# Moving the log1p series of a hybrid decoder kernel from GpSimd to VectorE

## The chip, the cores and the metric

The kernel runs on one NeuronCore of a Trainium2 chip. The metric is the device time of one launch in microseconds (us). A core has five engines with a queue each, and each works through its queue in order: TensorE (PE, matmuls), VectorE (DVE), ScalarE (ACT), GpSimd (POOL) and SyncE (SP, here only a queue that issues DMAs). They wait for one another by semaphores.

## The reference

One inference step of a two-layer recurrent decoder, for a prompt of 512 tokens and 8 sample tokens with shared weights. Layer 0 has an RG-LRU branch and a Mamba-2 branch behind one input projection; layer 1 is HGRN2. The parts that matter here are two softplus expressions of layer 0:

```python
log_a = -LRU_C * r * jax.nn.softplus(-lam.astype(F32))
dt = jax.nn.softplus(b_dt.astype(F32) + b_dt_bias.astype(F32))
a_neg = -jnp.exp(b_a_log.astype(F32))
acs = jnp.cumsum(dtc * a_neg.reshape(G_B, hg), axis=2)
```

lam has 1024 entries (128 partitions x 8), dt has 16 heads for each token (128 x 80: five blocks of tokens by 16 heads). softplus(x) is max(x, 0) + log1p(exp(-|x|)), and log1p(z) is worked out as twice a series in s = z / (z + 2): s (1 + s²/3 + s⁴/5 + ... + s¹⁶/17).

## The kernel before

All 520 tokens stand along the free dimension and features along the partitions. Each projection takes a 128-column tile of weights, loads it as float32, and splits it into a high part (fp32r, `whi`, a cast on ACT or DVE) and a residual (`wlo`, a subtraction on DVE); three products (`xnh` by `whi`, `xnl` by `whi`, `xnh` by `wlo`) of eight 128-blocks each make one tile, in two halves of 260 tokens. The order of layer 0's projections is: `ax` (8 tiles, the LRU's x), `xbc` (12 tiles, the Mamba x, B and C), `z`, `ag`, `z1`, then the output projections `oa` and `ob` and the gate `pg`. Layer 1 follows from about 450 us on.

Around these the small work is woven in. `evac_ax` (line 1116) copies an `ax` tile from PSUM into `bcs`, does the four-tap convolution into `xa` (prompt tokens on DVE; the sample tokens start with a scaling on POOL, line 1121, and go on with three fused steps on DVE), and calls `gates` (line 1092). `gates` splits `xa` into `xg`, multiplies it with the block-diagonal gate weights (the matmuls named `g`), and makes `lr`, `lg` and `lt` with ACT functions whose scale and bias are the LRU constants `c4` and `nc4` (in the tile `lamt`). `lru` (line 1131) takes the square roots and runs the recurrence as a scan on DVE.

`tables` (line 991) prepares the LRU constants: |lam|, a negation, an exp made exact by five squarings (`accurate_exp`, line 972), the series (`log1p_of`, line 956), the maximum, the sum and two scalings. `ssd_start` (line 1225) projects dt, takes |dt| and exp on ACT, runs the series, the maximum, the add and the product with `aneg` into `dA`, and sums `dA` along the tokens with a triangular matmul into `acs`; the whole chunked Mamba scan and the sample states (`ssd_chunk`, `ssd_sample`) hang on `acs`. In both places every step but the reciprocal stands on POOL.

The order in which instructions stand on each engine is not that of the code. Every call is recorded with a priority (the position of the projection at which it stands, shifted by `side(...)`), and the class `Plan` then works through all of them with a list of charges: it moves a clock of its own for each engine, gives each engine the ready instruction of the lowest priority number, and charges it. Lines 90 to 95 hold the charges that matter: DVE's fused step and tensor_tensor 0.067 + n/960 us, POOL's tensor_tensor 0.21 + n/480 and tensor_scalar 0.22 + n/1200, and `SYNC` (0.12 us, line 40) between a step and one that needs it. `later(4.0)` on line 1265 adds 4 us for TensorE work of `ssd_start` that waits for another engine. The chip then runs each queue in the order so found, whatever the true durations are. All of the instructions carry line 520 in the profile, since they are issued from there; they are told apart by their tiles. `dtt` holds dt's tiles, `htmp` the series' temporaries, `hb` holds `aneg`, `csm` is the sample part of the Mamba convolution, `smp` the sample states.

Of the kernel before, what the change touches and what calls it, by code (L numbers as in the profile page):

```python
# [21 lines left out]
MUL, ADD, SUB, MAX, MIN = ALU.mult, ALU.add, ALU.subtract, ALU.max, ALU.min  # L22
# [7 lines left out]
NH = 16  # L30
# [179 lines left out]
class Plan:  # L210
# [53 lines left out]
    @contextmanager  # L264
    def block(self, main=False):

        self.open = Op(self, self.pos + self.shift, 0)
        self.open.forms["pe"] = [[], 0.0, None]
        self.open.main = main
        self.open.ins, self.open.outs = [], []  # L270
        yield
        op, self.open = self.open, None
        op.forms["pe"][1] /= 2400.0
        self.add(op, op.ins, op.outs)
# [266 lines left out]
def hybrid_decode_step_kernel(ctx: ExitStack, tc: tile.TileContext, I, O, mode="both"):  # L541
# [19 lines left out]
    act, dve, pool, pe, sp = (Engine(plans, k) for k in ("act", "dve", "pool", "pe", "sp"))  # L561
    side, block = (lambda *a, **k: plans[-1].side(*a, **k)), (lambda *a: plans[-1].block(*a))

    def new(pool_, shape, tag, name, bufs=1, dt=F32):
        return plans[-1].tile(pool_, shape, dt, tag, name, bufs, {"psm": PSUM, "psa": PSUM, "drp": DRAM}.get(pool_, SBUF))
# [7 lines left out]
    def grab(name):  # L573

        return new("psa", [128, 512], "ax", name)
# [7 lines left out]
    def bc(ap, shape):  # L583
        return ap.to_broadcast(shape)

    def tt(out, a, b, op, eng=dve):
        eng.tensor_tensor(out=out, in0=a, in1=b, op=op)

    def stt(out, a, s, b, op0, op1):
        dve.scalar_tensor_tensor(out=out, in0=a, scalar=s, in1=b, op0=op0, op1=op1)  # L590

    def ts(out, a, s1, op0, s2=None, op1=None, eng=dve):
        if op1 is None:
            eng.tensor_scalar(out=out, in0=a, scalar1=s1, scalar2=None, op0=op0)
        else:
            eng.tensor_scalar(out=out, in0=a, scalar1=s1, scalar2=s2, op0=op0, op1=op1)

    def fn(out, in_, func, **kw):
        act.activation(out, in_, func, **kw)

    def copy(out, in_):

        plans[-1].record(("act", "copy", (out, in_), {}), ("dve", "tensor_copy", (out, in_), {}))
# [9 lines left out]
    def ltile(shape, name, dt=F32):  # L613
        return new("lay", shape, name, name, dt=dt)
# [147 lines left out]
    htmp = new("big", [128, 4160], "h", "htmp")  # L762
# [38 lines left out]
    def select(t, pattern, base, cm, fill):  # L801
        pool.affine_select(out=t, in_=t, pattern=pattern, compare_op=ALU.is_ge, fill=fill, base=base,
                           channel_multiplier=cm)
# [29 lines left out]
    def P1(r, n=1):  # L833
        return pt[:, 0, r:r + n]

    def P2(r, n=1):
        return pt[:, 1, r:r + n]
# [108 lines left out]
    lamt = ltile([128, 4, 8], "lamt")  # L946
    c4, nc4 = lamt[:, 2], lamt[:, 3]
    hbias = ltile([128, 16], "hbias")
    hcn = ctile([128, NH], "hcn")
    aneg = hb[:, 2, :]  # L950
# [2 lines left out]
    flag = ctile([1, 1], "flag", I32)  # L953
    fl = ctile([128, 4], "fl")

    def log1p_of(z, n, lo):

        t = htmp[:, lo:lo + 4 * n].rearrange("p (a b) -> p a b", a=4)
        s, s2, q, r = t[:, 0], t[:, 1], t[:, 2], t[:, 3]
        ts(s, z, 2.0, ADD, eng=pool)  # L960
        dve.reciprocal(q, s)
        tt(s, z, q, MUL, pool)
        tt(s2, s, s, MUL, pool)
        ts(q, s2, 1.0 / 17.0, MUL, 1.0 / 15.0, ADD, pool)
        for c in (13, 11, 9, 7, 5, 3, 1):
            tt(q, q, s2, MUL, pool)
            ts(q, q, 1.0 / c, ADD, eng=pool)
        tt(r, q, s, MUL, pool)
        ts(r, r, 2.0, MUL, eng=pool)
        return r  # L970

    def accurate_exp(t, k):

        fn(t, t, AF.Exp, scale=1.0 / (1 << k))
        for _ in range(k):
            tt(t, t, t, MUL, pool)

    def buffers():

# [11 lines left out]
    def tables():  # L991
        pool.memset(triu, 1.0)
        select(triu, [[1, 128]], 0, -1, 0.0)

        act.activation(lamt[:, 0], P1(56, 8), AF.Abs)
        ts(lamt[:, 0], lamt[:, 0], -1.0, MUL, eng=pool)
        accurate_exp(lamt[:, 0], 5)
        l1p_ = log1p_of(lamt[:, 0], 8, 320)
        ts(lamt[:, 1], P1(56, 8), -1.0, MUL, 0.0, MAX, pool)
        tt(lamt[:, 1], lamt[:, 1], l1p_, ADD, pool)  # L1000
        ts(c4, lamt[:, 1], -4.0, MUL, eng=pool)
        ts(nc4, lamt[:, 1], 4.0, MUL, eng=pool)
        ts(hbias, P1(40, 16), 0.5, MUL, eng=pool)
        ts(hcn, P2(64, 16), 0.5, MUL, eng=pool)

        ts(P1(64, 60), P1(64, 60), 0.5, MUL, eng=pool)

    def dt_tables():
        pool.tensor_copy(aneg, hb[:, 1, :])
        accurate_exp(aneg, 5)  # L1010
        ts(aneg, aneg, -1.0, MUL, eng=pool)
        copy(dtws[:, :, :NH], dtw)
        tt(dtws[:, :, NH:], dtw, dtws[:, :, :NH].bitcast(F32), SUB)
# [46 lines left out]
    with plans[-1].together(xnl[:, 3]):  # L1060
        with side(12.0):
            buffers()
            tables()
        with side(25.0):
            dt_tables()
        with side(40.0):
            lower_bounds()
# [122 lines left out]
    dt_raw, dt_z, dt, dA, nacs = (dtt[:, i] for i in range(5))  # L1190
# [12 lines left out]
    def dt_project():  # L1203


        ps = [grab(f"dt{h_}") for h_ in range(2)]
        with block():
            for k in range(KT):
                for x in (xnh, xnl):
                    for h_ in range(2):  # L1210
                        pe.matmul(ps[h_][:2 * NH, :HN], lhsT=dtws[:, k, :], rhs=x[:, k, h_ * HN:(h_ + 1) * HN],
                                  start=(k == 0 and x is xnh), stop=(k == KT - 1 and x is xnl))
        dth = htmp[:2 * NH, 1888:1888 + N]
        for h_ in range(2):
            copy(dth[:, h_ * HN:(h_ + 1) * HN], ps[h_][:2 * NH, :HN])
        psd = grab("dtT")
        with block():
            for i in range(5):
                t0 = i * 128 if i < 4 else N - 128
                pe.transpose(psd[:, i * 2 * NH:(i + 1) * 2 * NH], dth[:, t0:t0 + 128], ident[:2 * NH, :2 * NH])  # L1220
        d3, p3 = dt_raw.rearrange("p (i h) -> p i h", i=5), psd[:, :160].rearrange("p (i a h) -> p i a h", i=5, a=2)
        tt(d3, p3[:, :, 1], bc(hb[:, 0, :].unsqueeze(1), [128, 5, NH]), ADD)
        tt(d3, p3[:, :, 0], d3, ADD)

    def ssd_start():
        dt_project()
        act.activation(dt_z, dt_raw, AF.Abs)
        fn(dt_z, dt_z, AF.Exp, scale=-1.0)
        lg_ = log1p_of(dt_z, 80, 0)
        ts(dt, dt_raw, 0.0, MAX, eng=pool)  # L1230
        tt(dt, dt, lg_, ADD, pool)
        tt(dA.rearrange("p (i h) -> p i h", i=5), dt.rearrange("p (i h) -> p i h", i=5),
           bc(aneg.unsqueeze(1), [128, 5, NH]), MUL, pool)
        ps = grab("acs")
        with block():
            pe.matmul(ps[:, 0:64], lhsT=triu, rhs=dA[:, :64], start=True, stop=True)
            pe.matmul(ps[:, 64:128], lhsT=ones, rhs=dA[:, :64], start=True, stop=True)
        copy(at_[:, 0:2, :], ps[:, :128].rearrange("p (a b) -> p a b", a=2))
        ts(nacs[:, :64], acs, -1.0, MUL)
        tt(edt, alast, acs, SUB)  # L1240
        ps = grab("acsT")
        with block():
            pe.transpose(ps[:64, :128], acs, ident)
            pe.transpose(ps[:16, 128:256], dt[:, 64:80], ident)
            pe.transpose(ps[:16, 256:384], dA[:, 64:80], ident)
        copy(acsT, ps[:64, :128])
        copy(sdt[:, 0, :], ps[:16, 248:256])
        fn(sdt[:, 1, :], ps[:16, 376:384], AF.Exp)
        fn(edt, edt, AF.Exp)
        fn(eal, alast, AF.Exp)  # L1250
        sp.dma_start(out=acsT_d, in_=acsT)
        sp.dma_start(out=sdt_d, in_=sdt.rearrange("h a b -> h (a b)"))
        for e in range(2):
            sp.dma_start(out=sfm[e * 64:(e + 1) * 64].rearrange("p j a b -> p j (a b)"),
                         in_=sdt_d.rearrange("(j e) c -> e j c", e=2)[e].partition_broadcast(64))
# [9 lines left out]
    with side(DT_LATE), plans[-1].later(4.0):  # L1265
        ssd_start()
        lru_out()
# [997 lines left out]
```

## Time and profile before

| what | value |
|---|---|
| median of 3 runs | 1056.26 us (1055.57 to 1057.36) |
| the profiled execution | 1052.58 us, span 1050.9 us, mean granted clock 0.994 |
| PE | 1023.1 us, 97% of the span |
| DVE | 832.6 us, 79%, 1705 instructions |
| ACT | 630.8 us, 60%, 1482 instructions |
| POOL | 139.4 us, 13%, 241 instructions |

A row in order of time reads: start, duration, engine, line, operation, tile written <- tiles read, shapes (partitions x elements), count, and in brackets how long the engine had been idle and what ended that. A row of a group reads: busy time in all, mean ns of one, idle time ahead of it. Starts of DVE and ACT instructions overlap the ends of those before, so a duration is longer than the distance between two starts. A row of a stretch has the engines' busy times, and behind them the share of full speed that TensorE's clock was granted.

### The profile page before, as it was taken

Reading aid. Unit: us, or ns where it says so; the run is one execution under the profiler, and the core shown is the slowest. Engines: PE = TensorE matmul, PEld = TensorE weight load, DVE = VectorE, ACT = ScalarE, POOL = GpSimd, SP = SyncE. Lnnn points to the kernel's source line nnn. Section 1 sums busy time; section 2 is a strip of 40 time slices with the busy share of each in tenths; the row PEclk is TensorE's granted clock in tenths of the full one; section 3 lists DMA queues with packets and bytes.
Section 4 is the critical chain, followed back from the end, with each engine's and each line's share of the span. In section 5 each row is a group of like instructions: output and inputs, shape, how many; then the busy total and the mean of one; then the engine's idle time right before and its main releaser. Section 6 shows DMA issues by size and latency. Waiting matters only on the chain.

```text
span 1050.9 us, 21517 instructions
## 1 busy us (share of the span) xinstructions
PE 1023.1 (97%) x8427; PEld 1000.0 (95%) x8427; DVE 832.6 (79%) x1705; ACT 630.8 (60%) x1482; POOL 139.4 (13%) x241
## 2 busy tenths in 40 slices
PE   9989899999999999999999999999999999999995
PEld 8989899899999999999999999999999999999995
DVE  6789788998996656697989759698598979868853
ACT  6588876654673222365676726678268685764553
POOL 4635854100000000001000000001000000100000
PEclk9999999999999999999999999999999999999998
DMA  9712254336586223553353433433434443553311
GB/s 285 246 30 92 81 166 141 122 110 191 188 257 213 89 98 117 153 203 90 98 149 109 142 91 108 139 100 113 122 90 139 124 116 111 137 180 121 121 41 45
DMA packets 129957, 138.45 MB, mean 132 GB/s; under 512 B 13704, under 2 KB 111128, under 8 KB 129832
## 3 DMA queue, kind: packets, MB, share of 16 engines
q1 hardware_dynamic: 129464, 136.64, 42.6%
q8 instruction: 68, 1.11, 0.4%
q10 hardware_dynamic: 160, 0.30, 0.1%
q14 instruction: 41, 0.34, 0.1%
q0 software_dynamic: 224, 0.06, 0.0%
HBM read 111.71 MB, written 25.44 MB: 131 GB/s over the span
## 4 chain that ended last, share of the span: by engine, by line
PE 73%; DVE 10%; DMA 6%; ACT 4%; POOL 3%; issue 2%; SPq 0%; POOLq 0%; ACTq 0%; DVEq 0%
PE o L520 10%; PE sm L520 9%; PE q L520 9%; PE pg L520 9%; PE g L520 8%; PE ob L520 4%; PE sg L520 4%; PE xbc L520 2%; PE ax L520 2%; DVE wlo L520 2%; PE oa L520 2%; PE pl L520 2%; PE z L520 1%; DMA smp<-in_state_b_ssm_dram 1%; POOL csm L520 1%
## 5 line engine op out<-in xcount | busy, mean ns | idle before, releaser
L520 ACT CAST whir<-wraw 128x512 fp32r<-128x512 f32 (+1 forms) x121 | 96.3, 798 | 83.9 <-PE o L520 40.6
L520 DVE TENSOR_TENSOR wlor<-wraw,whir 128x512 fp32r<-128x512 f32 (+1 forms) x121 | 109.6, 910 | 12.5 <-ACT whir L520 12.1
L520 ACT CAST whi<-wraw 128x1024 fp32r<-128x1024 f32 (+1 forms) x56 | 57.8, 1032 | 48.6 <-PE ob L520 34.5
L520 POOL TENSOR_TENSOR at__1738<-at__1738,nhalf 128x4 f32<-128x4 f32 (+1 forms) x24 | 22.6, 942 | 461.5 <-DVE at__1738 L520 455.5
L520 DVE TENSOR_TENSOR wlo<-wraw,whi 128x1024 fp32r<-128x1024 f32 (+1 forms) x64 | 77.3, 1208 | 8.0 <-ACT whi L520 7.4
L520 PE MATMUL o<-ohl,whir 128*128 128x260 f32 x512 | 83.0, 284 | 0.0
L520 PEld LDWEIGHTS o<-ohl,whir 128*128 128x128 f32 x512 | 70.0, 188 | 0.9 <-issue 0.6
L520 PE MATMUL g<-xh,whir 128*128 128x260 f32 x256 | 54.6, 294 | 1.1 <-DVE l1a L520 1.1
L520 PE MATMUL q<-xh,whir 128*128 128x260 f32 x256 | 53.2, 289 | 0.0
L520 PE MATMUL q<-xh,wlor 128*128 128x260 f32 x256 | 51.5, 283 | 0.0
L520 PE MATMUL q<-xl,whir 128*128 128x260 f32 x256 | 51.4, 282 | 0.0
L520 PE MATMUL g<-xl,whir 128*128 128x260 f32 x256 | 51.4, 282 | 0.0
L520 PE MATMUL g<-xh,wlor 128*128 128x260 f32 x256 | 51.4, 282 | 0.0
L520 PE MATMUL o<-ohl,wlor 128*128 128x260 f32 x256 | 51.4, 282 | 0.0
L520 DVE TENSOR_TENSOR h<-h,o 128x520 f32<-128x520 f32 x40 | 27.8, 694 | 26.2 <-PE o L520 25.9
L515 ACT ACT_TABLE_LOAD x36 | 46.2, 1283 | 0.6
L520 PE MATMUL sm<-uh,whir 128*128 128x260 f32 x140 | 40.4, 289 | 1.8 <-DVE l1a L520 1.6
L520 PE MATMUL sm<-xh,whir 128*128 128x260 f32 x140 | 41.4, 296 | 0.0
L520 PEld LDWEIGHTS g<-xh,whir 128*128 128x128 f32 x256 | 39.2, 189 | 2.2 <-DVE l1a L520 1.3
L520 PE MATMUL sm<-xh,wlor 128*128 128x260 f32 x140 | 39.6, 283 | 0.3 <-DVE wlor L520 0.3
L520 PE MATMUL xbc<-xnh,whi 128*128 128x260 f32 x192 | 39.7, 289 | 0.0
L520 PE MATMUL sm<-xl,whir 128*128 128x260 f32 x140 | 39.6, 283 | 0.0
(609 smaller groups left out, 3594.2 us busy)
## 6 DMA issues: line engine op xcount, KB each, us to landing
wraw<-in_c_w_in_dram SPq DMA_DIRECT2D x32, 1024.0 KB
wraw<-in_ab_w_in_dram SPq DMA_DIRECT2D x15, 1024.0 KB
wraw<-in_ab_w_out_dram SPq DMA_DIRECT2D x8, 1024.0 KB
wraw<-in_ple_gate_dram SPq DMA_DIRECT2D x8, 1024.0 KB
wraw<-in_c_w_out_dram SPq DMA_DIRECT2D x8, 1024.0 KB
pl<-pl_d SPq DMA_DIRECT2D x2, 2080.0 KB
smp<-in_state_b_ssm_dram SPq DMA_DIRECT2D x8, 512.0 KB
acy<-acsT_d SPq DMA_DIRECT2D x8, 512.0 KB
```

The lines of the kernel that those rows point to most:

```text
L515: self.engines["act"].preload_act_table_set(SETS[table])
L520: getattr(f, name)(*a, **k)
```

## The change

`log1p_of`, which returned the logarithm, becomes `softplus_tail`, which adds it to a tile that already holds the maximum. Its Horner steps are fused: the product and the sum of one coefficient, two POOL instructions before, are one scalar_tensor_tensor on DVE, and the last doubling and the add are one as well. With the reciprocal it has 14 instructions. The maximum, dt's product with `aneg`, and in `tables` the negation, the squarings and the two scalings move to DVE too. `accurate_exp` takes the engine as an argument; its other two uses stay on POOL. Priorities, charges and the planner are as they were.

```diff
-    def log1p_of(z, n, lo):
-
-        t = htmp[:, lo:lo + 4 * n].rearrange("p (a b) -> p a b", a=4)
-        s, s2, q, r = t[:, 0], t[:, 1], t[:, 2], t[:, 3]
-        ts(s, z, 2.0, ADD, eng=pool)
-        dve.reciprocal(q, s)
-        tt(s, z, q, MUL, pool)
-        tt(s2, s, s, MUL, pool)
-        ts(q, s2, 1.0 / 17.0, MUL, 1.0 / 15.0, ADD, pool)
-        for c in (13, 11, 9, 7, 5, 3, 1):
-            tt(q, q, s2, MUL, pool)
-            ts(q, q, 1.0 / c, ADD, eng=pool)
-        tt(r, q, s, MUL, pool)
-        ts(r, r, 2.0, MUL, eng=pool)
-        return r
-
-    def accurate_exp(t, k):
+    def softplus_tail(dst, z, n, lo):
+
+        t = htmp[:, lo:lo + 3 * n].rearrange("p (a b) -> p a b", a=3)
+        s, s2, r = t[:, 0], t[:, 1], t[:, 2]
+        ts(s2, z, 2.0, ADD)
+        dve.reciprocal(r, s2)
+        tt(s, z, r, MUL)
+        tt(s2, s, s, MUL)
+        ts(r, s2, 1.0 / 17.0, MUL)
+        for c in (15, 13, 11, 9, 7, 5, 3):
+            stt(r, r, 1.0 / c, s2, ADD, MUL)
+        stt(r, r, 1.0, s, ADD, MUL)
+        stt(dst, r, 2.0, dst, MUL, ADD)
+
+    def accurate_exp(t, k, eng=pool):
 
         fn(t, t, AF.Exp, scale=1.0 / (1 << k))
         for _ in range(k):
-            tt(t, t, t, MUL, pool)
+            tt(t, t, t, MUL, eng)
...
         act.activation(lamt[:, 0], P1(56, 8), AF.Abs)
-        ts(lamt[:, 0], lamt[:, 0], -1.0, MUL, eng=pool)
-        accurate_exp(lamt[:, 0], 5)
-        l1p_ = log1p_of(lamt[:, 0], 8, 320)
-        ts(lamt[:, 1], P1(56, 8), -1.0, MUL, 0.0, MAX, pool)
-        tt(lamt[:, 1], lamt[:, 1], l1p_, ADD, pool)
-        ts(c4, lamt[:, 1], -4.0, MUL, eng=pool)
-        ts(nc4, lamt[:, 1], 4.0, MUL, eng=pool)
+        ts(lamt[:, 0], lamt[:, 0], -1.0, MUL)
+        accurate_exp(lamt[:, 0], 5, dve)
+        ts(lamt[:, 1], P1(56, 8), -1.0, MUL, 0.0, MAX)
+        softplus_tail(lamt[:, 1], lamt[:, 0], 8, 320)
+        ts(c4, lamt[:, 1], -4.0, MUL)
+        ts(nc4, lamt[:, 1], 4.0, MUL)
...
         dt_project()
         act.activation(dt_z, dt_raw, AF.Abs)
         fn(dt_z, dt_z, AF.Exp, scale=-1.0)
-        lg_ = log1p_of(dt_z, 80, 0)
-        ts(dt, dt_raw, 0.0, MAX, eng=pool)
-        tt(dt, dt, lg_, ADD, pool)
+        ts(dt, dt_raw, 0.0, MAX)
+        softplus_tail(dt, dt_z, 80, 0)
         tt(dA.rearrange("p (i h) -> p i h", i=5), dt.rearrange("p (i h) -> p i h", i=5),
-           bc(aneg.unsqueeze(1), [128, 5, NH]), MUL, pool)
+           bc(aneg.unsqueeze(1), [128, 5, NH]), MUL)
```

## The prediction

> **What bounds the kernel now.** The table of engines comes first, then the stretches: start and end, length, busy time of each engine, and behind these the clock granted to TensorE.
>
> ```profile
> PE 1023.1 (97%) x8427; PEld 1000.0 (95%) x8427; DVE 832.6 (79%) x1705; ACT 630.8 (60%) x1482; POOL 139.4 (13%) x241
> ```
>
> ```profile
> core 0: us, PE busy (x) PEld busy (x) DVE busy (x) ACT busy (x) POOL busy (x), PEclk, DMA share, GB/s
> 42.00:61.00 19.00, 15.93 (x124) 14.94 (x124) 13.30 (x33) 9.90 (x20) 14.10 (x38) 1.00 0.53 185
> 61.00:100.00 39.00, 39.00 (x325) 38.48 (x325) 35.91 (x76) 34.34 (x57) 16.26 (x23) 1.00 0.27 82
> 100.00:128.00 28.00, 24.73 (x206) 24.35 (x205) 20.79 (x28) 25.18 (x38) 22.09 (x45) 1.00 0.24 76
> 128.00:130.00 2.00, 2.00 (x16) 2.00 (x17) 1.43 (x5) 0.21 (x2) 0.31 (x2) 0.90 0.00 0
> 130.00:132.00 2.00, 2.00 (x11) 2.00 (x10) 2.00 (x4) 1.11 (x4) 0.89 (x1) 0.50 0.00 0
> 132.00:134.00 2.00, 2.00 (x14) 2.00 (x14) 2.00 (x3) 1.22 (x4) 2.00 (x1) 0.74 0.03 8
> 128.00:175.00 47.00, 47.00 (x384) 46.39 (x385) 40.63 (x62) 32.46 (x70) 22.41 (x34) 0.96 0.44 138
> 175.00:300.00 125.00, 122.93 (x1023) 115.48 (x1022) 116.49 (x234) 73.74 (x229) 11.09 (x17) 1.00 0.52 160
> 300.00:1050.00 750.00, 734.26 (x6091) 723.36 (x6089) 575.67 (x1223) 427.23 (x1018) 34.06 (x41) 0.99 0.41 124
> ```
>
> PE is the bound: all but 27.8 us of the span (1050.9 - 1023.1) are matmuls. A change can gain where PE stands still, and POOL's average of 13% hides that it is busy 14.10 of 19 us and 22.09 of 28 us in exactly the two stretches around the change, where PE loses 3.07 and 3.27 us. So I asked each engine's instructions, in order of time, what it waited for there. First the LRU constants (42 to 61):
>
> ```profile
> 41.12 0.24 POOL L520 TENSOR_SCALAR htmp<-lamt 128x8 f32<-128x8 f32 x1
> 54.75 1.22 POOL L520 TENSOR_SCALAR lamt<-lamt 128x8 f32<-128x8 f32 x2
> ```
>
> ```profile
> 51.75 0.25 DVE L520 SCALAR_TENSOR_TENSOR xa<-htmp,pt,xa 128x8 f32<-128x8 f32 x1 [2.90 <-POOL xa L520]
> 58.39 0.75 DVE L520 SCALAR_TENSOR_TENSOR lt<-vtmp,lt 128x520 f32<-128x520 f32 x1 [1.75 <-ACT vtmp L520]
> ```
>
> ```profile
> 50.82 0.86 ACT L520 ACTIVATE lg<-g,hbias 128x260 f32<-128x260 f32 x2
> 56.00 0.82 ACT L520 ACTIVATE lt<-lr,lamt 128x520 f32<-128x520 f32 x1 [4.33 <-POOL lamt L520]
> ```
>
> ```profile
> 48.33 1.58 PE L520 MATMUL g<-xg,gw 128*128 128x260 f32 x11 [0.37 <-DVE xg L520]
> 55.27 1.59 PE L520 MATMUL g<-xg,gw 128*128 128x260 f32 x11 [1.63 <-DVE xg L520]
> 59.71 0.36 PE L520 MATMUL g<-xg,gw 128*128 128x260 f32 x1 [0.71 <-DVE xg L520]
> 60.35 1.59 PE L520 MATMUL g<-xg,gw 128*128 128x260 f32 x11 [0.29 <-DVE xg L520]
> ```
>
> The series on POOL runs from 41.12 to 55.97. A sample-token start of xa (line 1121) stands behind it in POOL's queue; DVE, whose queue is in order, waits 2.90 us for that xa with the gate's input xg behind it, and PE stands 1.63 us at the gate matmul. Then ACT waits 4.33 us for the constants, DVE 1.75 us for what ACT makes of them, and PE 0.71 + 0.29 us more.
>
> The second stretch is dt:
>
> ```profile
> 106.22 0.42 POOL L520 TENSOR_SCALAR htmp<-dtt 128x80 f32<-128x80 f32 x1
> 127.46 0.36 POOL L520 TENSOR_TENSOR dtt<-dtt,hb 128x80 f32<-128x80 f32 x1
> ```
>
> ```profile
> 127.88 0.43 PE L520 MATMUL acs<-dtt,triu 128*128 128x64 f32 x2 [3.27 <-POOL dtt L520]
> ```
>
> From the first step at 106.22 to dA at 127.82 are 21.6 us on POOL; PE, which takes its matmuls in a fixed order, stands 3.27 us at acs with weights ready behind it. In the rows of 128 to 134 the granted clock is then 0.90, 0.50 and 0.74: (0.10 + 0.50 + 0.26) x 2 = 1.72 us of full speed lost behind that wait. No such dip follows the 1.63 us wait (clock 1.00 from 42 to 100). The Trainium skill (TensorE: Matmul & The Clock Gate, Part 1) says that about 3.4 us of idling halves the rate; the trace has 3.27 us and a half rate, and by either a wait cut well below that loses no clock.
>
> **The change part by part.** *Off POOL.* For dt 20 steps of the series, the maximum, the add and the product with aneg (23); for the constants the negation, five squarings, 20 steps, maximum, add and two scalings (30). What they cost there:
>
> ```profile
> L520 POOL TENSOR_SCALAR htmp<-htmp 128x80 f32<-128x80 f32 x9 | 5.6, 619 | 0.7
> L520 POOL TENSOR_TENSOR htmp<-htmp 128x80 f32<-128x80 f32 x9 | 5.1, 569 | 0.1
> L520 POOL TENSOR_TENSOR htmp<-htmp 128x8 f32<-128x8 f32 x9 | 3.7, 408 | 0.6
> L520 POOL TENSOR_SCALAR htmp<-htmp 128x8 f32<-128x8 f32 x9 | 3.1, 349 | 0.8
> ```
>
> About 24 us: 20 x 0.59 + 3 x 0.4 for dt, 30 x 0.38 for the constants. The planner charges POOL 0.38 and 0.29 us for an 80-wide step (lines 94 and 95), the rows say 0.57 and 0.62: that, with other POOL work between the steps, is why acs was ordered before its input was there, although ssd_start's PE work is already put 4 us after it (line 1265).
>
> *On to DVE.* Each reciprocal was there already. Added are 13 + 2 steps for dt and 13 + 9 for the constants, 37 in all. No 80-wide fused step stands in the trace; the nearest rows:
>
> ```profile
> 102.94 0.23 DVE L520 TENSOR_TENSOR dtt<-dtT,hb 128x80 f32<-128x80 f32 x1
> 103.09 0.74 DVE L520 SCALAR_TENSOR_TENSOR bcs<-bcs,pt 128x512 f32<-128x512 f32 x1
> 113.05 0.77 DVE L520 TENSOR_TENSOR lg<-lg,lt 128x520 f32<-128x520 f32 x1
> 113.86 1.22 DVE L520 TENSOR_TENSOR_SCAN xa<-lr,lg 128x512 f32<-128x512 f32 x1
> ```
>
> ```profile
> L520 DVE SCALAR_TENSOR_TENSOR bcs<-csm 128x8 f32<-128x8 f32 x2 | 0.2, 152 | 0.0
> L520 DVE RECIPROCAL htmp<-htmp 128x80 f32<-128x80 f32 x1 | 0.7, 652 | 0.9 <-POOL htmp L520 0.9
> ```
>
> An independent successor starts 0.15 us after an 80-wide step (102.94 to 103.09): low end 15 x 0.15 = 2.3 us. A successor that reads the result starts 0.04 us after its end (113.05 + 0.77 to 113.86): high end 15 x (0.23 + 0.04) = 4.1 us. For the 8-wide ones 22 x 0.10 to 22 x 0.19 = 2.2 to 4.2 us. I take the low ends plus a little, 2.6 and 2.9 us, since the planner offers DVE other work between dependent steps, and a step that starts late because nothing else was there costs no one anything.
>
> The Trainium skill (VectorE: DVE Perf Modes, The DRAIN you can't avoid) says that an operation starts only when the pipe behind the one before has emptied. By that the sum would take the high ends, 2.8 us more DVE time; the trace agrees for the dependent pair and not for the independent one.
>
> *The constants.* DVE is free 1.25 and 1.30 us ahead of 41.4 and 43.05, both times waiting for POOL:
>
> ```profile
> 41.39 0.20 DVE L520 RECIPROCAL htmp<-htmp 128x8 f32<-128x8 f32 x1 [1.25 <-POOL htmp L520]
> 43.05 0.23 DVE L520 SCALAR_TENSOR_TENSOR xa<-htmp,pt,xa 128x8 f32<-128x8 f32 x1 [1.30 <-POOL xa L520]
> ```
>
> That holds most of the 2.9 us; the rest falls into the 2.90 us hold that vanishes. The constants are then there by about 45 instead of 55.97, ahead of the first gate activations (ACT has them done at 51.7), so the 4.33 and 1.75 us waits go. PE gains 1.63 + 0.71 + 0.29 = 2.63 us; the 0.37 us at 48.33 I leave, as conv of the first tile now shares DVE with the series. If that cover fails, the gain sinks by at most the 2.9 us that it hides: -0.3 us is the low end.
>
> *dt.* The rows of ACT's exp and of DVE behind acs:
>
> ```profile
> 105.04 0.26 ACT L520 ACTIVATE dtt<-dtt 128x80 f32<-128x80 f32 x1
> ```
>
> ```profile
> 128.57 0.29 DVE L520 COPY at__1738<-acs 128x128 f32<-128x128 f32 x1 [3.66 <-PE acs L520]
> ```
>
> The chain can start at 105.3. If DVE put one operation of 0.74 us between any two steps, the chain would take 15 x (0.74 + 0.15) + 0.65 = 14 us and end at 119; with 1.22 us each time (the weight residuals) 21.2 us, at 126.5. PE comes to acs at 127.88 - 3.27 = 124.6 now. With DVE idle for over 7 us of 100 to 128 (20.79 of 28 busy) I take 119: the 3.27 us and the 1.72 us of clock both go, 4.99 us. Low end: with 126.5 about 1.9 us of wait stay and no clock dip, 3.1 us gained.
>
> *What is late next.* The sum is 2.63 + 4.99 = 7.6 us. Behind it, DVE has to be early too: from 128 to 175 it is busy 40.63 of 47 us, from 175 to 300 116.49 of 125, and there it feeds PE with weight residuals. Its removed idle time is 1.25 + 1.30 + 2.90 + 1.75 us in the first stretch and 3.7 us behind acs plus 0.9 us before the reciprocal, 11.8 us in all; less 5.5 us of new work it is 6.3 us earlier against PE's 7.6 us. So I take 1.3 us back in the stage bound by DVE: 6.3 us. Everything after 300 is PE at 734 of 750 us and carries the shift to the end. Against the profiled execution (span 1050.9, time 1052.58 us) that is 1046.3; the median of the runs shown is 3.68 us above that execution, so 1050.0 us.
>
> **Rivals.**
>
> *DVE eats it.* The chain on DVE runs into a queue that is full (35.91 of 39 us from 61 to 100), with the high ends, 8.3 us added: DVE is only 11.8 - 8.3 = 3.5 us earlier, and if its steps also delay a residual once or twice (1.2 us each), 1 to 2 us remain: 1054.5, hardly told from no change (a difference under 0.2%, 2.1 us, can't be told here). For it: DVE and ACT are nearly full from 61 to 100. Against: over 7 us idle just where dt's chain falls.
>
> *Slower, by a new hold in the sample states.* The planner lists all instructions by its charges, so other charges give other orders everywhere behind 34 us, not only here. The place where a worse order costs most is the Mamba sample states, 230 to 300, whose loads DVE and ACT take in order:
>
> ```profile
> DVE smp L520 <- DMA smp<-in_state_b_ssm_dram: 4.8, 3, 3.3
> ACT smp L520 <- DMA smp<-in_state_b_ssm_dram: 10.3, 3, 4.8
> ```
>
> These waits cost PE almost nothing today. If the new order puts a state's update ahead of a weight split that PE needs, each hold costs PE up to 4.8 us and, once past about 3 us, 1.7 us of clock. One eats 6.5 us, the whole forecast; from two on the kernel is slower: 7.6 - 13 = -5.4 us, 1061.7. With one and a half it is 1058.5. For it: DVE is at 93% there, and nothing ties the new order to the old. Against: the update depends on acs, PE and store alike, which all move together.
>
> *Half of it.* The planner, which now charges the chain 0.15 us a step, puts acs earlier in PE's order as well, and PE waits there again for 1 to 2 us with no dip, or only one of the two stretches pays: 2.6 to 4 us gained, 1052.9.
>
> **How the numbers follow.** Forecast (4 to 9 us gained) 0.46; more than 9 us, where POOL's emptier queue also frees the convolution's sample tail, 0.05; half of it 0.18; DVE eats it 0.14; slower 0.17. Faster by over 0.2%: 0.46 + 0.05 + 0.18 and 0.02 of DVE eats it, 0.71. Same: the 0.12 left of that; slower: 0.17. The likeliest case alone spans 1047 to 1052.5. For 8 in 10 the range reaches up to one and a half holds, 1058.5, and down to 11 us gained, 1045.
>
> **What would show it.** POOL falls by 53 instructions to about 188 and by some 24 us; DVE rises by 37 and 5 to 8 us. ACT's first lt no longer waits for lamt, PE no longer for xg between 50 and 61, and acs waits under 1 us with the clock at 1.00 behind it. The prediction is wrong if those waits are gone and the span isn't shorter (then the order behind 175 took it: look for new waits of PE between 175 and 340), or if acs still waits 3 us, now for DVE.

## The result and the profile after

The changed kernel takes 1048.7 us (median of 5 runs, 1046.5 to 1050.26) against 1057.36 us for the kernel before beside it (1055.57 to 1058.46), a ratio of 0.9917 with a 95% interval of [0.9896, 0.9939]. The profiled execution takes 1046.5 us, span 1044.7. The table of engines of the kernel after:

```profile
PE 1019.1 (98%) x8427; PEld 996.5 (95%) x8427; DVE 839.0 (80%) x1754; ACT 626.6 (60%) x1470; POOL 120.2 (12%) x188
```

POOL has the 53 instructions less that were counted, and DVE 6.4 us more of work. DVE's instructions rose by 49 and not 37: ACT has 12 fewer, copies and scalings that the kernel leaves to the planner to place on ACT or on DVE.

For the stages, PE's own landmarks are better bounds than fixed times: the first `ax` matmul, the first `z`, the first `oa`, and in layer 1, whose heads go in pairs, the transposes by `ident` of the sample outputs of heads 4 and 5 and of heads 8 and 9 (the stretch between these two is called "heads 6 and 7" here and in the expectations; it holds the sample steps of two pairs). The stretches of the kernel after (columns as in the prediction):

```profile
42.00:61.00 19.00, 19.00 (x160) 19.00 (x159) 17.58 (x56) 13.04 (x24) 4.26 (x8) 1.00 0.64 226
...
100.00:128.00 28.00, 28.00 (x236) 27.96 (x235) 27.81 (x50) 23.56 (x41) 19.73 (x29) 1.00 0.31 96
...
28.42:165.05 136.63, 135.28 (x1117) 133.65 (x1118) 126.54 (x259) 104.87 (x187) 62.40 (x98) 1.00 0.41 132
165.05:288.18 123.13, 121.94 (x1026) 114.54 (x1024) 115.64 (x231) 72.06 (x225) 13.30 (x21) 1.00 0.51 155
647.88:788.30 140.42, 137.16 (x1131) 134.03 (x1131) 110.41 (x258) 87.87 (x221) 6.14 (x6) 1.00 0.40 113
```

The same three stages of the kernel before:

```profile
26.85:171.47 144.62, 137.90 (x1117) 135.40 (x1118) 119.40 (x212) 108.68 (x198) 80.35 (x150) 0.99 0.39 126
171.47:295.45 123.98, 122.47 (x1027) 114.66 (x1025) 115.47 (x231) 72.15 (x225) 13.76 (x21) 1.00 0.50 154
655.76:794.13 138.37, 136.35 (x1132) 133.86 (x1131) 111.34 (x256) 88.79 (x223) 5.71 (x6) 1.00 0.40 115
```

PE no longer stands still in the two stretches around the change (19.00 of 19 us and 28.00 of 28), and the clock is 1.00 in every row. The stage from `ax` to `z` is 144.62 - 136.63 = 7.99 us shorter and the next one 0.85 us; heads 6 and 7 of layer 1 take 2.05 us longer. Of the rest, the first 27 us are 1.57 us longer, the stage of `oa` is 0.6 us shorter, and what is left agrees within 0.4 us.

What PE waits for from `ax` to `z`, in the kernel after (us in total, times, longest):

```profile
PE g L520 <- DVE xg L520: 0.8, 1, 0.8
PE g L520 <- DVE htmp L520: 0.4, 1, 0.4
```

and in the kernel before:

```profile
PE acs L520 <- POOL dtt L520: 3.3, 1, 3.3
PE g L520 <- DVE xg L520: 3.0, 4, 1.6
```

The wait at `acs` is gone and the ones for `xg` have shrunk from 3.0 to 0.8 us. (In the kernel after, PE also waits 1.69 us in front of the first `ax`, ahead of the stage, for a tile whose transfer landed later; before, that wait was 0.23 us. That is most of the 1.57 us of the start, and nothing of the change is computed there.) In order of time, PE finds `acs` ready, in DVE's queue the chain of dt looks like this, and the last DVE row before that is `dA`:

```profile
115.16 0.33 PE L520 MATMUL acs<-dtt,triu 128*128 128x64 f32 x2
```

```profile
97.32 0.20 DVE L520 TENSOR_SCALAR htmp<-dtt 128x80 f32<-128x80 f32 x1
...
100.43 0.25 DVE L520 TENSOR_TENSOR htmp<-dtt,htmp 128x80 f32<-128x80 f32 x1
100.71 0.24 DVE L520 TENSOR_TENSOR htmp<-htmp 128x80 f32<-128x80 f32 x1
100.98 0.20 DVE L520 TENSOR_SCALAR htmp<-htmp 128x80 f32<-128x80 f32 x1
...
103.45 0.23 DVE L520 SCALAR_TENSOR_TENSOR htmp<-htmp 128x80 f32<-128x80 f32 x1
103.61 0.74 DVE L520 SCALAR_TENSOR_TENSOR bcs<-bcs,pt 128x512 f32<-128x512 f32 x1
...
110.23 0.23 DVE L520 TENSOR_TENSOR dtt<-dtt,hb 128x80 f32<-128x80 f32 x1
```

The chain takes 97.32 to 110.46, 13.1 us where POOL took 21.6, and ends 4.7 us before PE comes to it. A step that reads the one before follows it by 0.27 us (100.43, 100.71, 100.98); one beside other work costs the queue 0.16 us (103.45 to 103.61).

### The profile page after: what moved, and what is told of

It is laid out like the page before. It is cut to its first block, busy times and chain, and to the rows that moved or that the text cites. A ratio compares the mean times of both kernels' runs of the same rounds, so it can differ in the third digit from the quotient of the medians.

```text
span 1044.7 us, 21506 instructions
## 1 busy us (share of the span) xinstructions
PE 1019.1 (98%) x8427; PEld 996.5 (95%) x8427; DVE 839.0 (80%) x1754; ACT 626.6 (60%) x1470; POOL 120.2 (12%) x188
## 4 chain that ended last, share of the span: by engine, by line
PE 84%; DVE 9%; ACT 2%; DMA 2%; issue 1%; SPq 0%; POOL 0%; POOLq 0%; ACTq 0%; DVEq 0%
PE o L520 10%; PE sm L520 10%; PE q L520 9%; PE pg L520 9%; PE g L520 8%; PE xbc L520 6%; PE ob L520 4%; PE ag L520 4%; PE sg L520 4%; PE z L520 4%; PE ax L520 3%; PE pl L520 1%; PE kv L520 1%; PE v L520 1%; PE A L520 1%
## 5 line engine op out<-in xcount | busy, mean ns | idle before, releaser
L520 PE MATMUL sm<-ul,whir 128*128 128x260 f32 x140 | 39.6, 283 | 0.0
```

Source lines behind the costliest of these rows:

```text
L520: getattr(f, name)(*a, **k)
```

## The experiments

The ratios below are each to runs of the kernel before on the same chip (medians 1056.61, 1056.68 and 1056.09 us on three occasions). The theory was the prediction's: POOL's two chains hold PE, one at `acs`, one through `xg`; without them the gains add up to the forecast. The rivals: one part alone does it; the order that the planner finds does it; a later place for `acs` would do as well; the sample start of `xa` standing behind the constants in POOL's queue is the cost, not the constants.

**The two parts apart.** The kernel after once more, then each half alone:

> The changed kernel once more, as the measure for the others of this call: 0.8% below the kernel before (8 to 9 us), with the last 40% of layer 1's heads in the new order.

Measured: 1046.57 us, ratio 0.9909 [0.989, 0.9928].

```diff
 # dt_only: ssd_start as after; tables() and log1p_of as before
-        ts(lamt[:, 0], lamt[:, 0], -1.0, MUL)
-        accurate_exp(lamt[:, 0], 5, dve)
+        ts(lamt[:, 0], lamt[:, 0], -1.0, MUL, eng=pool)
+        accurate_exp(lamt[:, 0], 5)
+        l1p_ = log1p_of(lamt[:, 0], 8, 320)
...
```

> dt's series, maximum, add and product on DVE; the LRU constants stay on POOL as before. PE's order is that of before, only acs stands 6 rows and acsT 6 rows earlier. Theory (the wait at acs and the clock behind it are the larger half): PE waits under 0.5 us at acs, clock 1.00 behind it, 4.5 to 5 us below before, and the waits for xg between 50 and 61 stay at 2.6 us. Rival (DVE eats it): the wait moves to PE's later stages, 0 to 2 us below before.

Measured: 1049.62 us, 0.9927 [0.9909, 0.9944]. The stage from `ax` to `z` and PE's waits in it:

```profile
27.61:168.90 141.29, 136.42 (x1119) 133.92 (x1119) 122.50 (x234) 103.60 (x187) 72.72 (x127) 1.00 0.40 128
```

```profile
PE g L520 <- DVE xg L520: 3.0, 4, 1.7
...
PE xbc L520 <- DVE wlo L520: 0.8, 1, 0.8
```

The wait at `acs` is gone, those for `xg` are untouched: the two chains are two causes. The stage is 144.62 - 141.29 = 3.3 us shorter. That is 1.7 us less than the 4.99 us of the wait and its dip. A new wait behind DVE at `xbc` (0.8 us) and a longer one at the second `ax` tile (1.0 us, 0.4 before; it stands ahead of the change) make up 1.4 us of that. The time fell by more than the 4.5 to 5 us expected, 7.7 us by the ratio: the stage explains less than half of it, and where the runs of before lose more than its first profile shows is taken up below.

```diff
 # lam_only: tables() as after; ssd_start as before
-        softplus_tail(dt, dt_z, 80, 0)
+        lg_ = log1p_of(dt_z, 80, 0)
+        ts(dt, dt_raw, 0.0, MAX, eng=pool)
+        tt(dt, dt, lg_, ADD, pool)
```

> The LRU constants on DVE; dt's series stays on POOL as before. In the planner's order acs stands 45 rows earlier on PE than before (row 374 against 419), since POOL's clock is emptier, while the real chain of 23 POOL steps still takes about 20 us. Theory: the waits for xg go (3.0 us), acs waits again for POOL, 2 to 5 us with the clock dip of 1.7 us, layer 1's new order costs 2 us: in all 0 to 2 us below before. Rival (the gain was POOL's queue, whichever part is taken off it): acs comes in time, 5 us or more below before.

Measured: 1055.58 us, 0.9995 [0.9983, 1.0008]: no change. Its row of PE's waits and the same stage:

```profile
PE acs L520 <- POOL dtt L520: 3.1, 1, 3.1
```

```profile
28.30:171.13 142.83, 137.42 (x1117) 135.35 (x1118) 123.92 (x239) 106.37 (x191) 70.28 (x121) 0.99 0.40 128
```

The waits for `xg` between 28 and 62 us are gone here, so the constants' half does its work, and the stage is 1.8 us shorter. But `acs` stands earlier in PE's order now (group 374 of its queue against 419), POOL's chain for dt still takes 20.7 us, and PE waits 3.1 us for it again, with the clock at 0.59 and 0.56 from 118 to 122. Heads 6 and 7 of layer 1 take 140.40 us here too, 2.03 us more than before. The parts do not add: 7.7 us for dt alone, 0.5 for the constants alone, 9.6 for both (each 1056.61 x (1 - ratio)). The kernel with dt alone has the old order in layer 1, the other two pay the 2 us of the new one.

**The order in layer 1.** Nothing of the change is computed in layer 1, but the kernel after and the one with the constants alone have the same new order there and the same 140.4 us. This kernel is the one after, with the planner's column count shifted in its phase late in its clock, so that layer 0 keeps the order of after and layer 1 gets back that of before:

```diff
+def late(t):
+    return 2.89 if t > 430.0 else 0.0
...
-                    c = c + 0.003 * len(calls) if cols[int(t / 3.41333) - 1] >= 3060 else 2.0 * c
-                    cols[int((t + c) / 3.41333)] += op.cols
+                    c = c + 0.003 * len(calls) if cols[int((t + late(t)) / 3.41333) - 1] >= 3060 else 2.0 * c
+                    cols[int((t + c + late(t)) / 3.41333)] += op.cols
```

> The changed kernel, with the planner's count of recent matmul columns shifted by 2.89 us of its own clock from 430 us on. It changes no instruction; layer 0 keeps the order of the changed kernel and layer 1's matmuls stand as in the kernel before. Theory (the other order of heads 6 and 7 costs 2.05 us between 648 and 788): 2 us below the changed kernel, that stage 138.4 us long as before. Rival (the 2 us are chance, transfers landing differently in one execution): within 0.5 us of the changed kernel, the stage again 140 us in it.

Measured: 1044.55 us, 0.9878 [0.9861, 0.9896], the fastest kernel of the study. Heads 6 and 7:

```profile
647.98:786.07 138.09, 136.26 (x1131) 133.77 (x1130) 111.16 (x256) 88.79 (x223) 5.72 (x6) 1.00 0.41 115
```

138.09 us with the old order, 140.42 with the new, everything else as in the kernel after: the order alone costs 2.3 us. Where, the order of time of PE in the kernel after shows:

```profile
680.99 1.13 PE L520 MATMUL A<-l1a 128*128 128x128 f32 x8 [0.46 <-DVE at__1639 L520]
684.96 0.39 PE L520 MATMUL os<-l1d 128*16 128x128 f32 x2 [0.98 <-DVE l1d L520]
```

The waits at `A` and `os` (1.4 us) are absent with the old order; a third, 0.95 us at `g`, is there in both. The other 0.9 us stand in PE's busy time (137.16 against 136.26 us for the same 1131 matmuls); what they are was not looked into. The two kernels' times do not overlap: 1042.83 to 1045.41 us here, 1045.55 to 1049.49 for the kernel after beside it.

**How far one profile of before can be trusted.**

> The kernel before, profiled a second time, since its profiled execution (1052.58 us) lies 4 us under its median and the changed kernel's gain is 6.1 us by the profiles and 9 to 10 us by the medians. Theory (the profile of before shows all there is): the stages from the first ax matmul on are as long as in the first profile within 0.3 us each, and only the 27 us ahead of it differ. Rival: the first stretch (ax to z, 144.62 us) is 2 to 4 us longer in this execution, since the wait at acs or the holds behind POOL vary from one execution to the next.

Measured: 1056.22 us, span 1054.4 against 1050.9 us, and the stages are

```profile
27.40:172.63 145.23, 138.92 (x1118) 136.62 (x1119) 119.42 (x212) 108.82 (x198) 80.45 (x150) 0.98 0.39 125
172.63:298.49 125.86, 122.65 (x1026) 114.77 (x1024) 115.44 (x231) 72.06 (x225) 15.62 (x21) 1.00 0.49 151
```

PE waits as before, 3.3 us at `acs` and 3.0 for `xg`. The clock behind `acs` stays low for longer:

```profile
128.00:130.00 2.00, 2.00 (x10) 2.00 (x11) 1.11 (x5) 0.00 (x0) 0.20 (x1) 0.50 0.00 0
130.00:132.00 2.00, 2.00 (x11) 2.00 (x10) 2.00 (x5) 1.04 (x3) 0.56 (x1) 0.50 0.00 0
132.00:134.00 2.00, 2.00 (x11) 2.00 (x11) 2.00 (x3) 1.50 (x4) 2.00 (x1) 0.50 0.03 8
```

Three stretches of 2 us at 0.50 are 3.0 us of full speed, where the first profile had 1.72. The spans differ by 3.5 us: 1.88 us from `z` to `oa`, 0.5 to 0.7 us in each of the stages up to `ax`, from `ax` to `z` and of `oa`; from `ob` on both executions agree within 0.3 us in every stage. Neither the theory nor the rival named that stage. So the profile that the prediction started from was a favourable execution of the same program, and against this one the kernel after gains 8.6 us from `ax` to `z` and 2.7 from `z` to `oa`.

What differs from `z` to `oa` is POOL again. Its rows for the sample convolution `csm` stand in front of a masked copy into `wsl` that ACT, then DVE, then PE wait for. First the first profile, then the second:

```profile
172.48 1.29 POOL L520 TENSOR_TENSOR csm<-LCb,pt 128x8 f32<-128x8 f32 x2
...
176.75 1.09 POOL L520 TENSOR_SCALAR_AFFINE_SELECT wsl<-acy 128x1024 f32<-128x1024 f32 x1
```

```profile
173.63 3.21 POOL L520 TENSOR_TENSOR csm<-LCb,pt 128x8 f32<-128x8 f32 x2
...
179.53 1.60 POOL L520 TENSOR_SCALAR_AFFINE_SELECT wsl<-acy 128x1024 f32<-128x1024 f32 x1
```

```profile
181.16 2.45 ACT L520 ACTIVATE wsl<-wsl,dtt 128x128 f32<-128x128 f32 x8 [3.80 <-POOL wsl L520]
```

```profile
190.22 0.27 PE L520 MATMUL sbt<-ident,sbc 128*16 128x128 f32 x1 [1.66 <-DVE acy L520]
```

POOL starts the copy 5.28 us after the first `z` in one execution and 6.90 in the other; ACT waits 1.65 against 3.80 us for it, and PE 0.87 at `sbt` against 1.66 there and 0.74 at `st`. All the profiles go this way: where POOL starts it 5.0 to 5.8 us after the first `z` (the first of before, the kernel after three times, one of them with the old order in layer 1, and three of the kernels below and above) the stage takes 123.1 to 124.0 us, and where it starts it after 6.9 to 7.4 us (five profiles) 125.3 to 125.9. This is a third hold behind POOL, which the change leaves in place. The traces show it; no edit removed it.

**A later place for acs, with the chain left on POOL.**

```diff
-        with side(DT_LATE), plans[-1].later(4.0):
+        with side(DT_LATE), plans[-1].later(8.0):
```

> The kernel before with 8 us instead of 4 us that the planner keeps between a step of ssd_start and TensorE's work that needs it; every step of the series stays on POOL. acs stands 18 rows later on PE (about 4.3 us of matmuls). Theory (PE lost time only because acs was ordered ahead of its input): the 3.27 us wait and the clock dip go, 3 to 5 us below before, and a quarter of a microsecond or so comes back at the chunk scan's start. Rival (the series itself is the chain): the scan and the sample states start later, DVE and PE wait for them between 165 and 300, and under 1.5 us are left.

Measured: 1056.31 us, 0.9993 [0.9975, 1.0011]. `acs` moved to group 437, at 133.9 us, and PE waits there all the same:

```profile
PE acs L520 <- POOL dtt L520: 2.8, 1, 2.8
```

```profile
108.40 0.42 POOL L520 TENSOR_SCALAR htmp<-dtt 128x80 f32<-128x80 f32 x1
...
133.49 0.36 POOL L520 TENSOR_TENSOR dtt<-dtt,hb 128x80 f32<-128x80 f32 x1
```

The delay also holds dt's transposes, so the chain starts 2.2 us later, and on POOL it runs 25.4 us instead of 21.6. PE also waits 1.5 us for `wsl` behind the scan (from `z` to `oa`), a wait that the first profile of before does not have. The rival is neither confirmed nor cleanly refuted, since the edit moved more than the place; it does show that this order knob could not buy what the faster chain did.

**What the constants cost: the hold in POOL's queue, or the constants.** In the kernel before, the sample start of `xa` stands behind the series on POOL. Two kernels take it to DVE: one from the kernel before, one with dt on DVE besides, both with the constants on POOL.

```diff
-            ts(s, LCa[:, 3:, j], P1(24 + j), MUL, P1(32 + j), ADD, pool)
+            ts(s, LCa[:, 3:, j], P1(24 + j), MUL, P1(32 + j), ADD)
```

> The kernel before with one edit: the scaling that starts xa's sample tokens goes from POOL to DVE (8 instructions); both series stay on POOL. acs stands at row 374 on PE as in the kernel with only the constants moved. Theory (PE's waits for xg came from xa standing behind the series in POOL's queue): the 1.63 us wait goes; ACT's wait for lamt stays at about 4 us and keeps 0.7 to 1.0 us of PE's waits; acs waits again, 2 to 4 us. Rival (the constants' lateness alone made PE wait): the waits for xg between 50 and 61 stay above 2 us.

> dt's part on DVE as in the changed kernel, and the start of xa's sample tokens on DVE; the LRU constants stay on POOL. acs and acsT stand on the same PE rows as in the changed kernel, layer 1 in its order too. Theory (the hold of xa was most of the constants' share): within 1.5 us of the changed kernel. Rival (the constants themselves must be early): PE waits 2 us or more for xg or g between 50 and 62, 2 to 4 us above the changed kernel.

Measured: 1059.63 us, 1.0028 [1.0009, 1.0047], slower, for the first; 1052.11 us, 0.9951 [0.9933, 0.9968] for the second, by the ratios 2.5 us behind dt alone and 3.6 to 4.4 behind the kernel after, as the rival had it. The intervals of the second and of dt alone overlap, and 2.3 us of the difference are layer 1's order: heads 6 and 7 take 140.41 us in the second and 138.14 with dt alone. In the first they take 140.39, PE waits 3.1 us at `acs`, and the clock dips at three places. One of them has no long wait in front of it:

```profile
52.86 0.36 PE L520 MATMUL g<-xg,gw 128*128 128x260 f32 x1 [0.88 <-DVE xg L520]
54.04 2.00 PE L520 MATMUL g<-xg,gw 128*128 128x260 f32 x11 [0.82 <-DVE xg L520]
```

```profile
54.00:56.00 2.00, 1.96 (x12) 1.96 (x13) 1.60 (x4) 1.19 (x2) 0.68 (x2) 0.75 0.00 0
56.00:58.00 2.00, 2.00 (x11) 2.00 (x10) 0.85 (x3) 1.97 (x5) 0.21 (x1) 0.50 0.00 0
58.00:60.00 2.00, 2.00 (x17) 2.00 (x17) 1.97 (x7) 2.00 (x5) 0.46 (x1) 0.90 0.00 0
```

Two waits of 0.88 and 0.82 us with one matmul between them cost (0.25 + 0.50 + 0.10) x 2 = 1.7 us of clock. DVE's waits in the second, from 28 to 62 us, show what the edit had left:

```profile
DVE xa L520 <- POOL LCa L520: 6.7, 2, 4.0
```

The copy of the tile's last columns (`LCa`, in `evac_raw`) stood on POOL in front of the moved instruction. So the hold was passed on to it, and these two kernels tell less than they were meant to. A third takes the copy to DVE too, and a fourth does the same to the kernel after:

```diff
-    def evac_raw(ps, i, lc):
+    def evac_raw(ps, i, lc, eng=pool):
-        pool.tensor_copy(lc, raw[:, T:T + 11])
+        eng.tensor_copy(lc, raw[:, T:T + 11])
-            raw = evac_raw(ps, j, LCa[:, :, j])
+            raw = evac_raw(ps, j, LCa[:, :, j], dve)
```

> dt's series on DVE, the constants on POOL as before, and both the halo copy LCa and the sample start of xa on DVE, so that nothing of the gates stands behind the series in POOL's queue. In dt_xa the copy had stayed on POOL and DVE waited 6.7 us for it, so that kernel had moved the hold by one instruction and not removed it. If the hold in POOL's queue was what the constants cost: DVE's waits for POOL between 28 and 62 go, PE's waits for xg fall to about 0.8 us as in the kernel after, and first ax to first z takes 136.6 to 138.5 us. If it is ACT, which needs the constants for its first lt: ACT's wait for lamt stays near 5 us, and first ax to first z stays at 140 to 142 us as in dt_only and dt_xa. In between means both.

> The kernel after, with the halo copy LCa and the sample start of xa on DVE too. In the kernel after DVE still waits 1.8 us in three pieces for POOL's xa between 28 and 62, and PE 0.8 us for xg and 0.4 for htmp. If these waits are all that POOL still costs there, first ax to first z gains at most 1.2 us (135.4 to 136.6). If DVE, which takes 16 more small instructions of 0.2 us, is the bound by then, it gets longer by up to 3 us. Heads 6 and 7 of layer 1 take 138.1 or 140.4 us according to the order that the planner finds, which no theory here predicts.

Measured: 1052.83 us, 0.996 [0.9943, 0.9976] for the third, 1049.55 us (1045.74 to 1052.31), 0.9944 [0.9925, 0.9962] for the fourth. The stage from `ax` to `z` in the second, the third and the fourth kernel:

```profile
28.03:169.79 141.76, 137.01 (x1119) 133.95 (x1118) 124.03 (x243) 105.32 (x188) 66.99 (x119) 1.00 0.39 126
```

```profile
29.40:169.23 139.83, 136.10 (x1119) 133.66 (x1118) 125.31 (x249) 104.00 (x188) 65.65 (x111) 1.00 0.40 128
```

```profile
26.55:164.08 137.53, 134.99 (x1119) 133.62 (x1118) 127.43 (x277) 101.09 (x183) 50.59 (x82) 1.00 0.41 131
```

In the third, DVE waits for nothing of the gates from POOL any more, and the stage falls by 1.9 us, from 141.76 to 139.83; 3.2 us to the 136.63 of after remain. PE still waits 1.6 us there for `xg` from DVE and 0.9 for `xg` from ACT. What remains of waits for POOL is mainly ACT's for the constants:

```profile
ACT lt L520 <- POOL lamt L520: 3.0, 1, 3.0
```

So in this stage both count, the hold with about 1.9 us and the constants with about 3.2, as far as single executions of kernels with different orders can be compared (two of the kernel before differ by 0.6 us in this stage). In the times, the third kernel has nothing of the 1.9 us (0.996 against 0.9951): its stage from `z` to `oa` takes 125.77 us, 123.31 in the second. In the fourth, DVE waits for nothing from POOL between 28 and 62 us and PE's waits for `xg` and `htmp` (1.2 us) are gone, and yet it gains nothing over the kernel after: its stage from `ax` to `z` is 0.9 us longer, and its ratio is 0.9944 where the kernel after has 0.9917 and 0.9909. The loss stands at `flag`, the check of layer 1's lower bounds, where PE now waits:

```profile
PE flag L520 <- DVE fl L520: 1.8, 1, 1.8
```

With 0.8 us more at a second matmul of `flag` that is 2.6 us; the kernel after has no wait there. Whether the new order or DVE's fuller queue makes `flag` late is not told apart. The profiled execution, with a span of 1044.0 us as short as that of after, is the fastest of the five; in which stage the longer runs lose the rest isn't known.

## Why the prediction was right, and where its steps were not

*The bound and the two places.* Right: the waits for `acs` and `xg` went, and with them most of the stage's idle time of PE (6.72 us before, 1.35 after) and the clock dip. The prediction's gross sum there was 7.6 us; the profiles give 7.99 against the first execution of before and 8.6 against the second. That the sum fits so well is in part luck: with dt alone the stage is 3.3 us shorter, where 4.99 were forecast, and the constants on top of it bring 4.7 more (141.29 - 136.63), where 2.63 were forecast.

*dt, 4.99 us.* Right in mechanism. The chain took 13.1 us where 14 were worked out, `acs` waits for nothing, and the clock behind it is 1.00. With dt alone 3.3 us of it show in that stage, 3.9 against the second execution. The dip of 1.72 us, one term of the sum, was the mild case: in the second execution the same wait cost 3.0 us of clock. And the prediction's rule that a wait cut well below 3.27 us loses no clock does not hold: two waits of under 0.9 us close together cost 1.7 us in the kernel with the start of `xa` on DVE.

*The constants, 2.63 us.* The waits went as said, but not by the step given. The constants were to be there "by about 45"; they are complete at 57.78, where before had them at 55.97 (counted from the first `ax`, 29.4 us against 29.1):

```profile
57.54 0.24 DVE L520 TENSOR_SCALAR lamt<-lamt 128x8 f32<-128x8 f32 x2
```

```profile
57.90 1.52 ACT L520 ACTIVATE lt<-lr,lamt 128x520 f32<-128x520 f32 x2
```

On DVE the planner spread the steps between other work over 17 us (from 40.41 on), and it moved ACT's first `lt` behind work that ACT had anyway, so ACT starts it at 57.90 without a wait. So the early constants played no part. The hold of `xa` in POOL's queue did, with 1.9 of the 5.1 us that the kernel with both dt and the start of `xa` on DVE lacks; the other 3.2 us come with the constants on DVE, and whether by ACT's order or by DVE's is not told apart.

*DVE's price, 5.5 us.* DVE's busy time rose by 6.4 us, with the 12 instructions in it that left ACT. The two prices of a step are both in the rows above, 0.16 us interleaved and 0.27 us in a dependent row. The Trainium skill (VectorE: DVE Perf Modes, The DRAIN you can't avoid) says that the next operation does not start until the pipe is empty, but that one that is not held starts earlier. The trace has both: in the dependent row the 0.24 us step at 100.71 is followed at 100.98, beside independent work a step of 0.23 us is followed after 0.16. The rival that DVE eats the gain is refuted for this order, but it is near: from 100 to 128 DVE is now busy 27.81 of 28 us.

*1.3 us handed back from 175 to 300.* Wrong: this term of the sum failed. The stage is 0.85 us shorter, or 2.7 against the second execution. The loss came at another place, 2.05 us in heads 6 and 7 of layer 1, through a mechanism that the prediction had only as a rival: the planner's charges give another order far behind the change. It named the sample states and 4.8 us a hold; the trace has two small waits in layer 1 (1.4 us together) and 0.9 us more busy time of PE, shown by the kernel that puts the order back.

*POOL's busy time* fell by 19.2 us and not by 24 (by 21.7 in the second profile of the kernel after).

*The shift from the profiled execution to the median, 3.68 us.* The forecast for a profile like the first was 1046.3 us, the profiled execution took 1046.5. That fit is luck: the stages from `ax` to `oa` gained 8.8 us and not 6.3, and layer 1's order and a later transfer at the start took 3.6 us of it back, neither of which the sum has. The forecast median was 1050.0, the measured one is 1048.7. The kernel after stands closer to its own profile than before did, and the stage that differed between the two profiles of before (123.98 and 125.86 us from `z` to `oa`) has 123.1 to 123.2 us in the three profiles with this order in layer 0. POOL's `csm` rows decide that, and not that dt is on DVE: the kernel with the copy on DVE has dt there too, starts `wsl` on POOL 7.40 us after the first `z`, and takes 125.77 us. Whether POOL's rows fall the short way in every run of the kernel after can't be told from its profiles alone.

*Half of it.* It did not come for both parts together, but the constants alone met just that mechanism: `acs` was ordered earlier and PE waits there again, 3.1 us.

## What to carry to other kernels

An engine with a small share of the span can set its length, when a chain of slow dependent steps on it lies ahead of something that the bound engine takes in a fixed order; ask which instructions stand behind the chain in its queue, and move them all, since one that is left takes over the hold (6.7 us at `LCa` here). Then look again, since moving them gives the planner another order: the kernel with all of them on DVE lost more at `flag` (2.6 us) than it gained at `xg` and `htmp` (1.2). In a kernel whose order comes from a list of charges, compare stage by stage between landmarks of the bound engine, far behind the change as well: here a fifth of the gain was lost 500 us later, and an edit to the order alone brought it back. And profile the kernel before twice: two executions of it differed by 3.5 us here, more than half of the 6.2 us by which the first profiles of before and after differ.

## What the runs showed of the hardware

POOL's time for one and the same small step is not fixed: the mean of the same nine steps was 619 ns in the kernel before and

```profile
L520 POOL TENSOR_SCALAR htmp<-htmp 128x80 f32<-128x80 f32 x9 | 7.3, 807 | 0.7
```

with the chain 2.2 us later, and one row of `csm` took 1.29 us and 3.21 us in two executions of the same program, where its neighbours take 0.35. What ends such a long row can be read from the two queues: behind the first `z` of five profiles (before twice, dt alone, the kernel after, the copy on DVE) the first run of long rows of `LCb` and `csm` ends 0.1 to 0.3 us after DVE begins `bx <- bx,dcol,yd`, which reads `yd` from PSUM, after a run of DVE steps on tiles in SBUF. So the long rows go with what DVE does beside them; the cause was not taken apart by an edit. A chain on POOL cannot be placed by one measured duration.

What a wait of about 3 us costs in clock is not fixed. Behind the 3.3 us at `acs` in the second profile of before it was 3.0 us of full speed, 1.72 in the first. Behind the 2.8 us of the later place for `acs` the clock was halved too:

```profile
134.00:136.00 2.00, 2.00 (x10) 2.00 (x10) 0.95 (x4) 1.98 (x6) 0.89 (x5) 0.50 0.04 8
136.00:138.00 2.00, 2.00 (x11) 2.00 (x11) 1.45 (x4) 0.87 (x3) 0.20 (x1) 0.50 0.00 0
```

so 2.8 us were enough here, where the Trainium skill (TensorE: Matmul & The Clock Gate, Part 1) has about 3.4 us of idling. Nor does the longest single wait decide it: single waits of 1.6 to 1.7 us left the clock at 1.00 (at `g` in the kernel before, at `sbt` in its second profile), but 0.88 and 0.82 us with one matmul between them halved it, as the rows of the kernel with the start of `xa` on DVE show.

The first 30 us differ from execution to execution with PE's order the same. The block of 48 projection matmuls ahead of `ax` starts at 20.23 us in the second profile of before and at 23.64 us in the kernel with the copy on DVE. In the latter, the stretch from 12 to 14 us has 10 matmuls where the kernel after has 20, at a granted clock of 1.00 in both. The same section of the Trainium skill says that the first matmuls run at half rate, and that how many do varies between runs of one kernel; the trace agrees that the rate at the start varies by a factor of two, but its column of the granted clock doesn't show it. It adds to the spread between the runs of one kernel, 2.6 to 8.6 us here.
